# GpSimd's drain moved behind its last load, its wait for the output, and one more row on TensorE, in a batched trace of matrix products

## The chip, the cores and the metric

The kernel runs on one core of one Trainium2 chip. The time is the device time of one execution in microseconds (us). The profile is one further execution, taken by the hardware profiler; its span runs from the first to the last instruction of the program.

## The reference

For eight pairs of 2176 x 2176 matrices of float32 the reference gives the trace of each product.

```python
B, N = 8, 2176
prod = np.matmul(a, b)
traces = np.diagonal(prod, axis1=1, axis2=2).sum(axis=-1)
return traces.astype(np.float32)
```

The trace of a product is the sum over all i, k of a[i, k] * b[k, i]. So no full product is needed: A has to be transposed, multiplied with B element by element, and summed up.

## The kernel before, in words

**Data.** Each matrix is 17 blocks of 128 rows (`NT` = 17). The 17 "rows" of a tile in SBUF, counted by `v` from 0 to 16, each hold 2176 bfloat16 numbers in each of 128 partitions. Rows 0 to 4 of a matrix (`MID` = 5) go to the tile `middle`, rows 5 to 16 (two groups of `SIDE` = 6) to `a_side` or `b_side`. `middle` takes A's part first and then B's. The tile `at` takes the whole transposed A. Nearly every load is issued by GpSimd (`nc.gpsimd.dma_start`), which lets the transfer turn float32 into bfloat16; one load of batch 0 and the store of the output are issued by SyncE (lines 138 and 147).

**A batch.** GpSimd loads A's middle, then A's sides, then B's middle (line 179) and B's sides (line 187), each when the buffer is free: it waits for semaphores on which TensorE and VectorE count what they have read. TensorE (PE) transposes A by matmuls with an identity (line 305) into three PSUM tiles; ScalarE (ACT) and VectorE (DVE, every fourth tile) copy these into `at` (line 216, in `evacuate`). When `at` is full, DVE multiplies and sums in one instruction (line 229, `multiply_reduce`): `at` rows 0 to 4 with `middle`, rows 5 to 16 with `b_side`. Both give one column of `sums`, a partial sum for each partition.

**The last batch.** B's sides do not come in one load. Rows 5 to 10 are one load (line 192, semaphore `b_all`), rows 11 and 12 (`piece0`), 13 (`piece1`), 14 (`piece2`) and 15 (`piece3`) are four (line 198), and row 16 comes in three pieces (line 203): columns 768 to 2175 (`piece4`), 256 to 767 (`piece5`) and 0 to 255 (`piece6`). These are the last instructions in GpSimd's stream. The work on them is divided by hand between two engines:

- DVE (lines 271 to 284) takes rows 0 to 4, rows 5 to 8 (`DVE_ROWS` = 4), row 14 (`DVE_ROW`), columns 1024 to 2175 of row 15 (`SHARED_ROW`, from `HALF` on), and columns 768 to 1407 of row 16. Then it waits for `traced` and takes the diagonal of PE's sum with an identity (line 284).
- PE (lines 313 to 346) takes rows 9 and 10, rows 11, 12 and 13, the first 1024 columns of row 15 and the rest of row 16. For each 128 columns it multiplies a block of `at` with the block of `b_side` and adds the 128 x 128 product in `trace_ps`; the diagonal of it is the part of the trace. Between the rows some matmuls without use (`KEEP_BUSY`, after rows 10, 12, 13 and 15, into a fill tile) keep it busy. Its last real matmul raises `traced`.

At the end PE sums the columns over the partitions with a matmul by ones (line 348), DVE adds these up (line 287, semaphore `reduced`), SyncE stores the result (line 147), and the store's landing raises `out` by 16.

**The order of the work.** All of it stands in one critical section (`tc.tile_critical()`, line 135): the semaphores are written by hand, and each engine runs its instructions in the order of the code. At the end of such a section each engine drains, that is, waits until it has finished what it was given, and SyncE waits for all of these drains; the profile puts these instructions down to line 135. A second critical section (lines 352 and 353) holds nothing but SyncE's wait for `out`. Behind it come the closing barriers of the program: each engine drains and reports, GpSimd gathers the reports and releases all, semaphores are cleared, and a second such round follows. The profile puts these down to line 379.

Of the kernel before, what the change touches and what calls it, by code (L numbers as in the profile page):

```python
# [10 lines left out]
def kernel(  # L11
# [6 lines left out]
    nc = tc.nc  # L18
# [12 lines left out]
    B_GROUPS = [(0, MID), (MID * P, SIDE), ((MID + SIDE) * P, SIDE)]  # L31
    LAST = MID + SIDE

    DVE_ROWS = 4
    LATE_SLICES = [(0, 2), (2, 1), (3, 1), (4, 1)]
    DVE_ROW, SHARED_ROW = LAST + 3, LAST + 4
    HALF = 8 * P
# [25 lines left out]
    sem = {}  # L63
# [15 lines left out]
    def group(src, start, g, m):  # L79

        rows = src[start:start + P * g * m, :]
        return rows.rearrange("(g p r) k -> p g (r k)", g=g, r=m)
# [49 lines left out]
    plain = b_side.bitcast(f32).rearrange("p r k -> p (r k)")[:, :N]  # L132
    half = N // 2

    with tc.tile_critical():  # L135

        first = a[0, 0:MID * P, :].rearrange("(p r) k -> p r k", r=MID)
        nc.sync.dma_start(out=plain, in_=first[:, MID - 1, :]).then_inc(sem["first"], 16)
        for bi in range(BATCH):
# [8 lines left out]
            out=out.rearrange("(a b) -> a b", a=1), in_=result[:1, :BATCH],  # L148
# [3 lines left out]
        for bi in range(BATCH):  # L152
            last = bi == BATCH - 1
            if bi == 0:
                nc.gpsimd.dma_start(
                    out=middle[:, 0:MID - 1, :].rearrange("p r k -> p (r k)"),
                    in_=first[:, 0:MID - 1, :].rearrange("p r k -> p (r k)"),
                ).then_inc(sem["a_mid"], 16)
            else:
                nc.gpsimd.wait_ge(sem["product"], 2 * bi - 1)  # L160
                nc.gpsimd.dma_start(  # L161
                    out=middle.rearrange("p (g r) k -> p g (r k)", g=1), in_=group(a[bi], 0, 1, MID),
                ).then_inc(sem["a_mid"], 16)
                nc.gpsimd.wait_ge(sem["filled"], per_batch * bi)
            nc.gpsimd.dma_start(  # L165
                out=a_side.rearrange("p (g r) k -> p g (r k)", g=2),
                in_=group(a[bi], MID * P, 2, SIDE),
            ).then_inc(sem["a_all"], 16)
            if bi == 0:
                for t in (identity32, identity16):  # L170
                    nc.gpsimd.memset(t, 0.0).then_inc(sem["cleared"], 1)
                for k, t in enumerate((identity32, identity16)):
                    nc.gpsimd.wait_ge(sem["cleared"], 2)
                    nc.gpsimd.affine_select(
                        out=t, in_=t, compare_op=mybir.AluOpType.not_equal, fill=1.0, base=0,
                        pattern=[[-1, P]], channel_multiplier=1,
                    ).then_inc(sem["constant"], 1)
            nc.gpsimd.wait_ge(sem["filled"], per_batch * bi + mid_fills)
            nc.gpsimd.dma_start(  # L179
                out=middle.rearrange("p (g r) k -> p g (r k)", g=1), in_=group(b[bi], 0, 1, MID),  # L180
            ).then_inc(sem["b_mid"], 16)
            if bi:
                nc.gpsimd.wait_ge(sem["product"], 2 * bi)
            else:
                nc.gpsimd.wait_ge(sem["cast"], 2)
            if not last:
                nc.gpsimd.dma_start(  # L187
                    out=b_side.rearrange("p (g r) k -> p g (r k)", g=2),
                    in_=group(b[bi], MID * P, 2, SIDE),
                ).then_inc(sem["b_all"], 16)  # L190
                continue
            nc.gpsimd.dma_start(
                out=b_side[:, 0:SIDE, :].rearrange("p (g r) k -> p g (r k)", g=1),
                in_=group(b[bi], MID * P, 1, SIDE),
            ).then_inc(sem["b_all"], 16)
            rows = b[bi, LAST * P:N, :].rearrange("(p r) k -> p r k", r=SIDE)
            for k, (r, m) in enumerate(LATE_SLICES):
                nc.gpsimd.dma_start(  # L198
                    out=b_side[:, SIDE + r:SIDE + r + m, :].rearrange("p r k -> p (r k)"),
                    in_=rows[:, r:r + m, :].rearrange("p r k -> p (r k)"),  # L200
                ).then_inc(sem[f"piece{k}"], 16)
            for k, (lo, mid, hi) in enumerate(LAST_PIECES):
                nc.gpsimd.dma_start(  # L203
                    out=b_side[:, MOST - 1, lo:hi], in_=rows[:, SIDE - 1, lo:hi],
                ).then_inc(sem[f"piece{len(LATE_SLICES) + k}"], 16)


        def evacuate(engine, copy, bi, dve):
# [12 lines left out]
            out=middle[:, MID - 1, :half], in_=plain[:, :half]  # L221
# [12 lines left out]
        def rows_product(v0, rows, acc):  # L234

            m = rows.shape[1]
            return multiply_reduce(
                at[:, v0:v0 + m, :].rearrange("q v x -> q (v x)"),
                rows.rearrange("q v x -> q (v x)"), acc,
            )  # L240
# [4 lines left out]
            out=middle[:, MID - 1, half:], in_=plain[:, half:]  # L245
        ).then_inc(sem["cast"], 1)
        for bi in range(BATCH):
# [12 lines left out]
            out=result[:1, 0:BATCH - 1],  # L260
# [5 lines left out]
        def column():  # L266
            nonlocal cols
            cols += 1
            return late_acc[:, cols - 1:cols]

        rows_product(0, middle, column())
        nc.vector.wait_ge(sem["b_all"], 16 * BATCH)
        rows_product(MID, b_side[:, 0:DVE_ROWS, :], column())
        slot = SIDE - LAST
# [4 lines left out]
        for k, (lo, mid, hi) in enumerate(LAST_PIECES):  # L279
# [8 lines left out]
            out=result[:1, BATCH - 1:BATCH], in_=total[:, early:early + cols],  # L288
# [26 lines left out]
        def multiply_on_pe(landed, v, lo, hi):  # L315

            row = b_side[:, v - MID, :]
            for c in range(lo, hi, P):
                work.append((landed, at[:, v, c:c + P], row[:, c:c + P], True))
# [5 lines left out]

        for v in range(MID + DVE_ROWS, LAST):
            multiply_on_pe(("b_all", 16 * BATCH), v, 0, N)
# [21 lines left out]
            total[:, early:early + cols], ones, late_acc[:, 0:cols], start=True, stop=True,  # L349
        ).then_inc(sem["summed"], 1)  # L350

    with tc.tile_critical():
        nc.sync.wait_ge(sem["out"], 16)


# [1 line left out]
_INS = ['a', 'b']  # L357
# [26 lines left out]
```

## Time and profile before

| what | value |
|---|---|
| median of 3 runs | 712.53 us (712.15 to 712.57) |
| the profiled execution | 713.01 us |
| its span, first to last instruction | 710.9 us |
| mean granted TensorE clock | 0.655 |
| DVE busy | 382.2 us (54%) |
| PE busy | 205.3 us (29%) |
| ACT busy | 202.4 us (28%) |
| GpSimd (POOL) busy | 25.0 us (4%) |
| moved by DMA | 152.13 MB, 214 GB/s in the mean |

The profiled execution's own time is 2.1 us more than its span: that is what lies around the program. The page gives the span in 40 slices, with the busy share of each engine, of the DMA engines and the granted clock; the chain that ended last follows the work back from the last instruction that counts as work. The timeline lists instructions in order of time, with the idle time of the engine before them and what ended it. Drains, branches and semaphore instructions do not count as busy time; they are found under the line that they are put down to, with shortest, median and longest duration in ns and the first and last start in us. There an engine's name has a q (POOLq, SPq) for the engine's queue.

### The profile page before, as it was taken

What the parts mean: (1) busy time and instruction counts of PE and PEld (TensorE: products, weight loads), DVE (VectorE), ACT (ScalarE), POOL (GpSimd) and SP (SyncE); (2) the same over time, 40 slices, a digit from 0 to 9 for tenths busy, and PEclk for the clock granted to TensorE, in tenths of its full rate; (3) what the DMA queues carried; (4) which work ended last, traced back from release to release, by engine and by line L of the source; (5) the groups of instructions that cost most, each with busy time, mean ns of one, the idle gap of its engine ahead of it and who ended that gap; (6) DMA issues with size and microseconds to landing.
All of it is one profiled execution on the core that took longest, in us unless ns stands there. A gap on an engine that the chain in (4) does not pass through costs nothing. (4 is left out here: it accounts for less than half of the span.)

```text
span 710.9 us, 3916 instructions
## 1 busy us (share of the span) xinstructions
PE 205.3 (29%) x1624; PEld 186.2 (26%) x1626; DVE 382.2 (54%) x96; ACT 202.4 (28%) x158; POOL 25.0 (4%) x47
## 2 busy tenths in 40 slices
PE   0335013450134401243013520126201261013744
PEld 0334012440124301243012520126201261013732
DVE  0105488154961639616395173952739427393386
ACT  1427002370034600445004540045400472004720
POOL 1000000000000000000000000000000000002000
PEclk9859555695567855678555775567755586555878
DMA  9999999999999999999999999999999999999995
GB/s 232 215 215 220 215 207 229 215 206 226 211 215 225 211 224 214 213 224 214 220 219 213 221 216 215 220 216 208 229 212 212 226 207 222 217 211 221 217 207 100
DMA packets 7687, 152.13 MB, mean 214 GB/s; under 512 B 643, under 2 KB 899, under 8 KB 1411
## 3 DMA queue, kind: packets, MB, share of 16 engines
q0 software_dynamic: 7536, 150.96, 99.1%
q1 hardware_dynamic: 146, 1.11, 0.5%
q8 instruction: 2, 0.03, 0.0%
q14 instruction: 3, 0.02, 0.0%
HBM read 303.04 MB, written 0.00 MB: 426 GB/s over the span
## 5 line engine op out<-in xcount | busy, mean ns | idle before, releaser
L216 ACT COPY at<-fill 128x1536 bf16<-128x1536 bf16 (+3 forms) x156 | 200.0, 1371 | 472.2 <-DVE sums L229 356.7
L229 DVE CUSTOM_DVE_ANT_0 at<-at,b_side 128x26112 bf16<-128x26112 bf16 (+4 forms) x11 | 205.1, 18665 | 83.5 <-DMA b_side<-in_b_dram 83.5
L216 DVE COPY at<-fill 128x1536 bf16<-128x1536 bf16 (+2 forms) x52 | 83.9, 1614 | 221.0 <-PE fill L305 220.6
L305 PE MATMUL fill<-identity,middle 128*128 128x128 f32 (+1 forms) x440 | 68.3, 339 | 371.2 <-PEq L303 371.2
L305 PEld LDWEIGHTS fill<-identity,middle 128*128 128x128 f32 (+1 forms) x440 | 63.2, 180 | 376.1 <-issue 375.7
L305 PE MATMUL fill<-identity,a_side 128*128 128x128 f32 (+1 forms) x1056 | 123.6, 276 | 114.3 <-PEq L303 113.7
L305 PEld LDWEIGHTS fill<-identity,a_side 128*128 128x128 f32 (+1 forms) x1056 | 113.5, 167 | 124.4 <-issue 124.0
L229 DVE CUSTOM_DVE_ANT_0 at<-at,middle 128x10880 bf16<-128x10880 bf16 x8 | 91.9, 11490 | 11.0 <-ACTq L217 11.0
L179 POOL DMA_DIRECT2D middle<-in_b_dram x8 | 4.5, 562 | 334.3 <-PE fill L305 334.3
L161 POOL DMA_DIRECT2D middle<-in_a_dram x7 | 3.9, 563 | 294.4 <-DVE sums L229 294.4
L342 PE MATMUL trace_ps<-b_side,at 128*128 128x128 bf16 x105 | 8.7, 249 | 10.5 <-DMA b_side<-in_b_dram 10.4
L342 PEld LDWEIGHTS trace_ps<-b_side,at 128*128 128x128 bf16 x105 | 7.6, 115 | 12.6 <-DMA b_side<-in_b_dram 12.4
L165 POOL DMA_DIRECT2D a_side<-in_a_dram x8 | 5.7, 711 | 0.0
L187 POOL DMA_DIRECT2D b_side<-in_b_dram x7 | 5.0, 712 | 0.0
L342 PE MATMUL fill<-at 128*128 128x512 bf16 x19 | 4.8, 379 | 0.1
L244 DVE CAST middle<-b_side 128x1088 bf16<-128x1088 f32 x1 | 0.7, 727 | 5.0 <-DMA b_side<-in_a_dram 5.0
L342 PEld LDWEIGHTS fill<-at 128*128 128x128 bf16 x21 | 1.9, 98 | 1.5
L220 ACT CAST middle<-b_side 128x1088 bf16<-128x1088 f32 x1 | 1.1, 1098 | 3.9 <-DMA b_side<-in_a_dram 3.9
L198 POOL DMA_DIRECT2D b_side<-in_b_dram x4 | 2.1, 563 | 0.0
L203 POOL DMA_DIRECT2D b_side<-in_b_dram x3 | 1.6, 593 | 0.0
L220 ACT ACT_TABLE_LOAD x1 | 1.3, 1283 | 0.9 <-SPq L135 0.9
L229 DVE DVE_READ_ACCUMULATOR2_ANT sums<- 128x1 f32 x14 | 1.2, 82 | 0.0
(17 smaller groups left out, 4.2 us busy)
## 6 DMA issues: line engine op xcount, KB each, us to landing
a_side<-in_a_dram POOLq DMA_DIRECT2D x8, 6528.0 KB, 54.6
b_side<-in_b_dram POOLq DMA_DIRECT2D x7, 6528.0 KB, 52.5
middle<-in_b_dram POOLq DMA_DIRECT2D x8, 2720.0 KB, 22.2
middle<-in_a_dram POOLq DMA_DIRECT2D x7, 2720.0 KB, 24.6
b_side<-in_b_dram POOLq DMA_DIRECT2D x1, 3264.0 KB, 36.3
middle<-in_a_dram POOLq DMA_DIRECT2D x1, 2176.0 KB, 14.9
b_side<-in_b_dram POOLq DMA_DIRECT2D x3, 544.0 KB, 45.2
b_side<-in_a_dram SPq DMA_DIRECT2D x1, 1088.0 KB, 5.2
```

The costliest lines, as they stand in the source:

```text
L161: nc.gpsimd.dma_start(out=middle.rearrange("p (g r) k -> p g (r k)", g=1), in_=group(a[bi], 0, 1, MID),).then_inc(sem["a_mid"], 16)
L165: nc.gpsimd.dma_start(out=a_side.rearrange("p (g r) k -> p g (r k)", g=2), in_=group(a[bi], MID * P, 2, SIDE),).then_inc(sem["a_all"], 16)
L179: nc.gpsimd.dma_start(out=middle.rearrange("p (g r) k -> p g (r k)", g=1), in_=group(b[bi], 0, 1, MID),).then_inc(sem["b_mid"], 16)
L187: nc.gpsimd.dma_start(out=b_side.rearrange("p (g r) k -> p g (r k)", g=2), in_=group(b[bi], MID * P, 2, SIDE),).then_inc(sem["b_all"], 16)
L198: nc.gpsimd.dma_start(out=b_side[:, SIDE + r:SIDE + r + m, :].rearrange("p r k -> p (r k)"), in_=rows[:, r:r + m, :].rearrange("p r k -> p ...
L203: nc.gpsimd.dma_start(out=b_side[:, MOST - 1, lo:hi], in_=rows[:, SIDE - 1, lo:hi],).then_inc(sem[f"piece{len(LATE_SLICES) + k}"], 16)
L216: copy(out=dst, in_=src).then_inc(sem[f"free{i % BUFS}"], 1)
L220: nc.scalar.copy(out=middle[:, MID - 1, :half], in_=plain[:, :half]).then_inc(sem["cast"], 1)
L229: return nc.vector.tensor_tensor_reduce(out=x if out is None else out, in0=x, in1=y, scale=1.0, scalar=0.0, op0=MUL, op1=ADD, accum_out=acc,)
L244: nc.vector.tensor_copy(out=middle[:, MID - 1, half:], in_=plain[:, half:]).then_inc(sem["cast"], 1)
L305: done = nc.tensor.transpose(into, block, identity)
L342: done = nc.tensor.matmul(trace_ps if real else fill_tiles[0][:, 0:4, :], x, y, start=(n == 0 or not real), stop=(n == len(work) - 1 or no ...
```

## The change

The change has two parts. `DVE_ROWS` goes from 4 to 3, so row 8 of the last batch is multiplied by PE, as its first row behind the wait for `b_all` (line 326), and no longer by DVE (line 273). And the end is arranged anew: the section is told not to drain GpSimd (`no_gpsimd_drain=True`), GpSimd gets a drain and a wait for `out` of its own behind its last load, and the second section with SyncE's wait goes away.

```diff
-    DVE_ROWS = 4
+    DVE_ROWS = 3
...
-    with tc.tile_critical():
+    with tc.tile_critical(no_gpsimd_drain=True):
...
                 nc.gpsimd.dma_start(
                     out=b_side[:, MOST - 1, lo:hi], in_=rows[:, SIDE - 1, lo:hi],
                 ).then_inc(sem[f"piece{len(LATE_SLICES) + k}"], 16)
+        nc.gpsimd.drain()
+        nc.gpsimd.wait_ge(sem["out"], 16)
...
-    with tc.tile_critical():
-        nc.sync.wait_ge(sem["out"], 16)
-
```

## The prediction, made before the changed kernel ran

> **What bounds the kernel now.** I read the page first, then the chain that ended last, then the timeline of the last 25 us, and last the instructions behind the kernel's last line, which count as no work and so hardly stand on the page. The page says what the first 700 us hang on.
>
> ```profile
> span 710.9 us, 3916 instructions
> DMA  9999999999999999999999999999999999999995
> GB/s 232 215 215 220 215 207 229 215 206 226 211 215 225 211 224 214 213 224 214 220 219 213 221 216 215 220 216 208 229 212 212 226 207 222 217 211 221 217 207 100
> ```
>
> Every slice but the last has the DMA engines busy at 90% or more. So up to the last landing at 702.95 us (semaphore events of the trace) no engine's work counts but what delays a load; the change moves no load. It can only act behind the last loads, and there are two pieces of that. The first is DVE's, from the chain (start us, us, what):
>
> ```profile
> 691.42 9.14 DVE at L229
> ...
> 700.57 2.34 DVE at L229
> ...
> 702.92 1.27 DVE at L229
> ...
> 704.20 0.74 DVE at L229
> ...
> 704.94 0.20 DVE diagonal L229
> ```
>
> These are the products of rows 5 to 8 (8704 elements a partition), row 14 (2176), 1152 columns of row 15, 640 columns of row 16, and the diagonal of PE's sum. They follow one another without a gap, although the data are there earlier: piece2 landed at 697.64, piece3 at 700.21, piece4 at 701.92, and PE had finished ("traced") at 703.30. DVE is 1.5 us behind everything it waits for.
>
> The second piece lies behind the output's issue at 705.62. The chain ends there, but the span has 5.3 us more. The instructions put down to the section's line 135 say why (duration ns min/median/max, first and last start):
>
> ```profile
> L135 SPq NOP  x2: 13/13/13, 0.7 to 709.3; - x2
> L135 ACTq DRAIN  x1: 14/14/14, 706.0 to 706.0; - x1
> L135 POOLq DRAIN  x1: 3250/3250/3250, 706.0 to 706.0; - x1
> L135 DVEq DRAIN  x1: 19/19/19, 706.0 to 706.0; - x1
> ```
>
> All engines drain at 706.0, when SyncE has issued the output; ACT and DVE take 0.02 us, GpSimd 3.25. SyncE's waits name it as well: "SPq L135" waited 3.0 us for "POOLq L135", once. Meanwhile the output landed at 706.68, 1.06 us after its issue (semaphore events), so its wait costs nothing now. Then come the second section and the closing barriers:
>
> ```profile
> L379 POOLq DRAIN  x3: 34/34/112, 709.3 to 710.7; - x3
> L379 SPq DRAIN  x3: 7/7/7, 710.0 to 710.3; - x3
> ```
>
> GpSimd's next drain, right behind the long one, takes 34 ns: the long one's work is done once. SyncE comes through the second section from 709.37 to 710.0 (its lines 352 and the barrier's first SyncE drain), and from its arrival at the barrier to the last instruction it is 710.1 to 710.9, 0.82 us.
>
> **Part 1, row 8 to TensorE.** DVE loses 2176 of 8704 elements. Slope of the chain's rows: (9.14 - 2.34) / (8704 - 2176) = 1.042 ns an element, so three rows take 9.14 - 2.27 = 6.87 us. Step by step: row 14 starts at 691.42 + 6.87 = 698.29 (piece2 is there since 697.64); row 15's part at 700.63 (piece3 at 700.21); that ends at 701.90, when piece4 is just landing, 701.92, with some 0.05 for the wait 701.97; row 16's part ends at 702.71. Now PE is late: "traced" comes at 703.30, and the diagonal starts at 703.34 where it started at 704.86. Of 2.27 us taken from DVE, 1.52 come out at the end.
>
> PE gains 17 matmuls and as many weight loads, between row 8's place and row 9, behind the same wait for b_all (687.2).
>
> ```profile
> 687.22 3.72 PE L342 MATMUL trace_ps<-b_side,at 128*128 128x128 bf16 x34 [7.50 <-DMA b_side<-in_b_dram]
> 690.99 1.46 PE L342 MATMUL fill<-at 128*128 128x512 bf16 x6
> 693.06 2.07 PE L342 MATMUL trace_ps<-b_side,at 128*128 128x128 bf16 x34 [0.61 <-DMA b_side<-in_b_dram]
> ...
> 700.26 0.62 PE L342 MATMUL trace_ps<-b_side,at 128*128 128x128 bf16 x8 [1.59 <-DMA b_side<-in_b_dram]
> ```
>
> The granted clock is 0.54 in 687.2 to 691.0 and 1.00 after 691; 34 matmuls take 3.72 us at the one and 2.07 at the other. Seventeen more cost 1.04 to 1.86 us. Idle time in front of piece0 (0.61) and piece3 (1.59 by the timeline) is 2.2 us together, so even the dearer figure is gone by 700.26: it costs nothing at the end. What follows 700.26 is paced by the landings of pieces 3 to 6. If that cover were gone, each us that PE comes late at "traced" would be one us at the end. Bounds of part 1: 0 (PE late by 1.5) and 1.52 (PE can't end before piece6, which landed at 702.95).
>
> **Part 2, the drain and the sections.** Moved: one GpSimd drain, from 706.0 to behind the last load's issue, which ends at 654.57 + 0.60 = 655.2. It stands in front of nothing but the new wait: GpSimd issues no load after it, so it is moved past no queue's work. Added: GpSimd's wait for the output. Behind that wait stand GpSimd's share of the section's end and of the closing barriers, and every engine waits for those. Removed: the section's 3.25 us drain and the second section, 0.64 us of SyncE.
>
> How long the early drain takes no row shows. At the short end it has done its work for the earlier loads long before 703 and ends with the last landing, 702.95, or a little behind it; at the long end it starts its 3.25 us only there and ends at 706.2. A gain below nothing is excluded for the drain itself: no load waits for it, so its start can bring nothing forward. I take the short end: the long drain of before ran when all had landed for 3.07 us, so its time is work of GpSimd's own and no waiting, and 47.8 us lie between 655.2 and 702.95 to do it in. Either way GpSimd then waits for the output.
>
> Sum: the output is issued at 705.62 - 1.52 = 704.10 and lands 1.06 later, 705.16. From there through GpSimd's wake-up and SyncE's arrival at the barrier I estimate 0.25 us (GpSimd's semaphore instructions at the end stand 0.08 apart, SyncE's 0.07; three or four of them; bounds 0.1 and 0.4), and 0.82 to the end: 706.2 against 710.9. That is 4.7 us, of which part 1 has 1.5 and part 2 3.2.
>
> The profiled execution took 713.01 us, 2.1 more than its span, which I leave as it is: 708.3. The runs shown have a median of 712.53 us, 0.5 less; by those 712.53 - 4.7 = **707.8 us**.
>
> **A rule against the change.** In the trace GpSimd's issues at 562.45 and 563.00 took 562 and 711 ns beside a DVE copy that took its usual 1491, so neither held the other; a drain beside a DVE instruction does not occur. The Trainium skill, "SBUF — State Buffer", summary of rules for kernel authors, says that of a DVE operation with two SBUF inputs and a GpSimd operation that reads SBUF the later one fully blocks until the first is done. If a waiting drain counted as such an operation, DVE's products would be held until 703 and the time would be that of the fourth rival; if it does not, the sum above stands. The drain's row is listed under GpSimd's queue and names no tile, which speaks for the second.
>
> **Rivals.** One: the drain's 3.25 us begin only with the last landing. It ends at 706.2, 1.04 behind the output, and the same 0.25 + 0.82 follow: span 707.3, time 708.9. For it: one drain is all the trace has, and it ran after all landings. Against it: its length shows no waiting.
>
> Two: the drain's cost comes back, because the closing barrier's drain, which now follows GpSimd's wait, pays it again. Then 705.16 + 0.1 + 3.25 + 0.1 + 0.82 = 709.4, a gain of 1.5: 711.0. Against it: the 34 ns of the second drain.
>
> Three: part 1 gives nothing, as PE comes 1.5 us later. That needs the slow clock for longer: at 0.54 all through, the 51 matmuls take 51 x 0.109 = 5.6 us and the next 34 another 3.7. Then only part 2's 3.2 us remain: 709.3. Against it: the clock rose at 691 under the same load.
>
> Four, the one that ends slower: the drain holds DVE. From 655.2 on DVE has 4 x 1.76 + 0.96 us of copies and 11.4 + 6.9 + 2.3 + 1.3 + 0.7 of products, 31 us, nearly all of which would run behind 703: a span of about 736, a time of about 737. For it: no row shows a drain beside a DVE instruction. Against it: GpSimd's issue and DVE's copy at 562 went side by side at their usual lengths. It decides from the point where DVE is held over 4.7 us longer than the loads hold it.
>
> **How the numbers follow.** Forecast 0.71; one 0.13; two 0.05; three 0.07; four 0.04. The forecast's own bounds are 707.5 (0.1 us in place of 0.25, and a few hundredths) to 708.0 (0.4), and runs of before scatter by 0.4. The range 707.2 to 709.2 holds the forecast and rival one, 0.84; rival three's 709.3 is just outside. A measurement can tell 0.2%, 1.4 us, from no change. Faster by that: the forecast, one, three and half of two, 0.94; within it the other half of two, 0.02; slower 0.04.
>
> **What would show it.** Right: no long GpSimd drain behind the output's issue, the drain at 655.2 ending near 703, no instruction of a second section, DVE's diagonal at 703.3 and behind a wait for PE, the output issued at 704.1, 2.1 us from there to the span's end. PE's idle time before piece3 shrinks, the landings stay. Wrong: a drain that ends at 706 (one), a long drain in the closing barrier (two), "traced" well behind 703.3 (three), or DVE's copies behind 655 starting late (four).

## The result, and the profile after

The changed kernel takes 708.68 us (median of 6 runs, 708.49 to 709.28) against 712.55 (712.15 to 713.08, 6 runs). The ratio is 0.9945 with a 95% interval of 0.9933 to 0.9958: 3.9 us less, between 3.0 and 4.8. The forecast was 707.8 with a range of 707.2 to 709.2. The profiled execution took 708.71 us with a span of 706.6.

The chain that ended last (start us, us, what) no longer runs through DVE's products. From the last loads on it is this ("issue" is time in which the engine waited for nothing that the profile shows):

```profile
652.90 49.87 DMA b_side<-in_b_dram
702.77 0.05 issue
702.82 0.69 PE trace_ps L344 x6
703.51 0.02 issue
703.53 0.29 DVE diagonal L231
...
703.88 0.21 PE total L350 x2
704.09 0.02 issue
704.12 0.15 DVE result L289
```

The loads, PE on the last pieces as they land, and then the few short steps that can't begin earlier. DVE's timeline says the same from its side; the brackets hold its idle time and what ended it:

```profile
691.21 6.95 DVE L231 CUSTOM_DVE_ANT_0 at<-at,b_side 128x6528 bf16<-128x6528 bf16 x1
...
698.09 2.42 DVE L231 CUSTOM_DVE_ANT_0 at<-at,b_side 128x2176 bf16<-128x2176 bf16 x1
...
702.14 0.83 DVE L231 CUSTOM_DVE_ANT_0 at<-at,b_side 128x640 bf16<-128x640 bf16 x1 [0.34 <-DMA b_side<-in_b_dram]
...
703.53 0.29 DVE L231 CUSTOM_DVE_ANT_0 diagonal<-identity,trace_ps 128x128 bf16<-128x128 f32 x1 [0.56 <-PE trace_ps L344]
```

The product of three rows takes 6.95 us where that of four took 9.22, and DVE now waits twice: 0.34 us for piece4, 0.56 us for PE. On PE:

```profile
687.06 5.30 PE L344 MATMUL trace_ps<-b_side,at 128*128 128x128 bf16 x51 [7.49 <-DMA b_side<-in_b_dram]
692.42 1.46 PE L344 MATMUL fill<-at 128*128 128x512 bf16 x6
693.71 2.06 PE L344 MATMUL trace_ps<-b_side,at 128*128 128x128 bf16 x34
...
700.46 0.62 PE L344 MATMUL trace_ps<-b_side,at 128*128 128x128 bf16 x8 [1.14 <-DMA b_side<-in_b_dram]
```

With row 8, PE's first rows take 5.30 - 3.72 = 1.58 us more. The idle time in front of piece0's rows is gone, and that in front of piece3's has become 1.14 us; PE is still ahead of the loads.

Behind the output's issue (704.29) the instructions of the section's line are (duration ns min/median/max, first and last start us):

```profile
L135 SPq NOP  x2: 13/13/13, 0.7 to 705.6; - x2
...
L135 POOLq NOP  x1: 13/13/13, 705.5 to 705.5; - x1
```

In GpSimd's place in the section's end stands a NOP (an instruction that does nothing) of 13 ns instead of a drain of 3250. GpSimd's drain is found under its own line, and its drains in the closing barriers are short:

```profile
L206 POOLq DRAIN  x1: 52200/52200/52200, 652.6 to 652.6; - x1
...
L378 POOLq DRAIN  x3: 34/41/112, 705.6 to 706.3; - x3
```

By the record it lasts from 652.61 to 704.81. Its start can't be taken to the tenth: the last load's issue, which stands before it in the stream, is recorded only from 653.42 to 654.02. What follows rests on its end alone. The last piece landed at 703.17 and the output at 705.36 (semaphore events), so the drain ends 1.64 us behind the last load and 0.55 us before the output is there.

### The profile page after: what moved, and what is told of

Read it like the earlier page. It is cut to its first block, busy times and chain, and to the rows that moved or that the text cites. A ratio compares the mean times of both kernels' runs of the same rounds, so it can differ in the third digit from the quotient of the medians.

```text
span 706.6 us, 3944 instructions
## 1 busy us (share of the span) xinstructions
PE 207.3 (29%) x1641; PEld 188.0 (27%) x1643; DVE 380.2 (54%) x96; ACT 202.3 (29%) x158; POOL 25.0 (4%) x47
## 3 DMA queue, kind: packets, MB, share of 16 engines
q0 software_dynamic: 7536, 150.96, 99.7%
## 5 line engine op out<-in xcount | busy, mean ns | idle before, releaser
L231 DVE CUSTOM_DVE_ANT_0 at<-at,b_side 128x26112 bf16<-128x26112 bf16 (+4 forms) x11 | 202.9, 18460 | 84.1 <-DMA b_side<-in_b_dram 84.1
L344 PE MATMUL trace_ps<-b_side,at 128*128 128x128 bf16 x122 | 10.3, 253 | 9.4 <-DMA b_side<-in_b_dram 9.3
L344 PEld LDWEIGHTS trace_ps<-b_side,at 128*128 128x128 bf16 x122 | 9.3, 116 | 11.3 <-DMA b_side<-in_b_dram 10.9
```

Of the source, the lines that this page charges most:

```text
L231: return nc.vector.tensor_tensor_reduce(out=x if out is None else out, in0=x, in1=y, scale=1.0, scalar=0.0, op0=MUL, op1=ADD, accum_out=acc,)
L344: done = nc.tensor.matmul(trace_ps if real else fill_tiles[0][:, 0:4, :], x, y, start=(n == 0 or not real), stop=(n == len(work) - 1 or no ...
```

## The experiments

**The two parts alone.** First row 8 on TensorE with the old end:

```diff
-    DVE_ROWS = 4
+    DVE_ROWS = 3
```

> The kernel before with row 8 of the last batch on TensorE, its end left as it was. My theory: the two parts add up, and this part is worth what the last landing allows. In the changed kernel the diagonal starts at 703.5 where before had 704.9, so 1.3 us less: about 711.2 us against 712.5, the 3.25 us drain following the output's issue as before. Rival: the long drain's end hangs on the last landing (it ended 6.3 us behind it before), so an earlier output gains nothing: 712.5.

Measured: 711.46 us against 712.72, ratio 0.9984 (0.9975 to 0.9994), 1.3 us less. The diagonal waits for PE, the output is issued at 704.48, and the section's drain moved with it:

```profile
703.72 0.29 DVE L229 CUSTOM_DVE_ANT_0 diagonal<-identity,trace_ps 128x128 bf16<-128x128 f32 x1 [0.55 <-PE trace_ps L342]
...
L135 POOLq DRAIN  x1: 3250/3250/3250, 704.9 to 704.9; - x1
```

Its length is the same, and it ended 4.8 us behind the last landing (703.35) where it ended 6.3 us behind it before. So it does not hang on the last landing. The rival falls.

This run also shows how thin PE's cover is. The granted clock was 0.50 from 687.5 to 693.2, so all 51 matmuls of rows 8 to 10 ran at the slow clock and took 5.62 us, as rival three supposed for them; 0.30 us of PE's idle time were left in front of piece3's rows.

Then the new end with four rows on DVE:

```diff
-    DVE_ROWS = 3
+    DVE_ROWS = 4
```

> The changed kernel with rows 5 to 8 on DVE again. My theory: the output is issued at 705.6 and lands at 706.7 as before, the early drain is over by then, and the changed kernel's 0.39 + 0.78 us follow: span 707.9, 3.0 us less than before, about 709.5 us. Rival (the drain still holds the end for some of its time): 710.5 or more.

Measured: 709.89 us, ratio 0.9958 (0.9945 to 0.9972), 2.8 us less; span 708.0 where 707.9 was expected. The output lands at 706.77 and the span ends 1.21 us later, as in the changed kernel. The rival falls. The two parts together, 1.3 + 2.8 = 4.1 us, are what both give at once, 3.9, within the intervals.

**Which piece of the new end does it?** Only the drain is added to the kernel before:

```diff
                 ).then_inc(sem[f"piece{len(LATE_SLICES) + k}"], 16)
+        nc.gpsimd.drain()
```

> The kernel before with nothing but GpSimd's own drain added behind its last load; the section's own drain, the second section and row 8 on DVE stay. My theory: the section's drain shrinks to some 0.04 us, SyncE comes to its wait for the output before 706.68, and 1.35 us follow from there as before: span 708.0, 2.9 us less, about 709.6 us. So the second section is worth only some 0.2 us. Rival (each section's drain pays its 3.25 us anew): 712.5, no change.

Measured: 709.98 us, ratio 0.9959 (0.9946 to 0.9973), 0.4 us above the expected figure, with a span of 708.1 where 708.0 was expected. The section's own drain, still there, has nothing left to do:

```profile
L135 POOLq DRAIN  x1: 41/41/41, 706.1 to 706.1; - x1
```

So one added line has all of part 2 that the times can tell. By the profiles the span ends 1.34 us behind the output's landing here and 1.21 with the new end: the second section and SyncE's wait are worth 0.13 us.

The counterpart takes only this line out of the changed kernel:

```diff
-        nc.gpsimd.drain()
         nc.gpsimd.wait_ge(sem["out"], 16)
```

> The changed kernel without its own drain behind the last load; GpSimd only waits for the output. My theory: the drain's work is then paid by the closing barrier, and behind the output's landing, not beside it: 3.2 us more than the changed kernel, span about 709.7, about 711.9 us, with a GpSimd drain of about 3.25 us at line 378 or so. Rival (the cost belongs to the section's kind of drain, and the closing one is short as always): 708.7, like the changed kernel.

Measured: 711.57 us (712.72 before, ratio 0.9985, 0.9976 to 0.9994), 2.9 more than the changed kernel. The closing barrier now pays; its GpSimd drains are:

```profile
L377 POOLq DRAIN  x3: 40/112/3250, 705.4 to 709.3; - x3
```

The longest of the three is the first; it begins 0.27 us behind the output's landing (705.18). This kernel is no better than row 8 alone (711.46): leaving out the section's drain gains nothing by itself. In each of these runs the next drain in GpSimd's stream pays, whichever it is.

**What the drain's length is made of.** These runs are read for their drains and landings; each is one execution. Four batches in place of eight, the old end (the result's tile keeps its eight places and is set to zero first):

```diff
-    BATCH, N, N2 = a.shape
+    ALL, N, N2 = a.shape
+    BATCH = 4
...
```

> The kernel before with four batches in place of eight (the last four traces are left at zero), so 23 loads on GpSimd's queue in place of 39 and about half the bytes; the old end. It is for the length of the section's GpSimd drain alone. A price for each load (3.25 us / 39 = 0.083) gives 1.9 us; a price by bytes or descriptors 1.6 us; a fixed price 3.25 us.

```profile
L136 POOLq DRAIN  x1: 1938/1938/1938, 356.6 to 356.6; - x1
```

The same bytes in more loads:

```diff
-            nc.sync.wait_ge(sem["a_all"], 16 * (bi + 1))
+            nc.sync.wait_ge(sem["a_all"], 32 * (bi + 1))
...
-            nc.gpsimd.dma_start(
-                out=a_side.rearrange("p (g r) k -> p g (r k)", g=2),
-                in_=group(a[bi], MID * P, 2, SIDE),
-            ).then_inc(sem["a_all"], 16)
+            for g in range(2):
+                nc.gpsimd.dma_start(
+                    out=a_side[:, g * SIDE:(g + 1) * SIDE, :].rearrange("p (g r) k -> p g (r k)", g=1),
+                    in_=group(a[bi], (MID + g * SIDE) * P, 1, SIDE),
+                ).then_inc(sem["a_all"], 16)
```

> The kernel before with each load of A's sides split into two loads: 47 loads in place of 39, the same bytes; the old end. For the length of the section's GpSimd drain. A price for each load gives 3.9 us; a price by bytes, or a fixed one, 3.25 us.

```profile
L135 POOLq DRAIN  x1: 3903/3903/3903, 706.1 to 706.1; - x1
```

23, 39 and 47 loads give 1.938, 3.250 and 3.903 us: (3.250 - 1.938) / 16 = 0.082 and (3.903 - 3.250) / 8 = 0.082 us for each load, and 0.05 on top. Bytes and a fixed price are out. So is a price by packets: GpSimd's queue moved 7536 with 39 loads and 7664 with 47, 2% more, and the drain is 20% longer.

A drain in the middle, in front of batch 4's first load:

```diff
                 nc.gpsimd.wait_ge(sem["product"], 2 * bi - 1)
+                if bi == BATCH // 2:
+                    nc.gpsimd.drain()
```

> The kernel before with one more GpSimd drain in the middle, in front of batch 4's first load, when 16 of the 39 loads have been issued; the old end. For the length of the section's drain. If a drain's price counts only the loads since the drain before, 23 x 0.082 + 0.05 = 1.94 us; if it counts all loads of the program, 3.25 us again. The drain in the middle waits for batch 3's last load and holds batch 4's first load back, so the time itself should be some 2 to 4 us longer, by a gap in the loads.

```profile
L135 POOLq DRAIN  x1: 1930/1930/1930, 710.5 to 710.5; - x1
```

Only the 23 loads since the drain before count. The one in the middle (from 341.98 on) ended at 354.20, 0.70 us behind the only load that was still under way (353.50). The time, 716.13 us beside 713.11 in one run each, shows what such a drain costs where loads stand behind it: some 3 us. The output was issued 4.4 us later (710.11 for 705.74), and the shorter drain at the end gave 1.3 us back.

**The early drain's remainder.** The changed kernel with four batches:

> The changed kernel with four batches in place of eight (the last four traces are left at zero). For the early drain's end: it came 1.64 us behind the last landing in the changed kernel. If that remainder is a fixed price behind the last landing, 1.6 us again; if it is a part of a price that grows with all the loads, about half, 0.8 us; if it belongs to the last loads alone (nine in flight), 1.6 us too.

Its drain ended at 355.03, 0.99 us behind the last landing at 354.05. So the remainder belongs neither to the last loads, which are the same, nor is it fixed. With the drain in the middle there are three points, 16, 23 and 39 loads with 0.70, 0.99 and 1.64 us: 0.041 us for each load. About half of a drain's price can't be done early; it comes behind the last landing and grows with all loads since the drain before, those included that had long landed. (The expected 0.8 us was half of 1.64 us; by the loads it should have been 23/39 of it, 0.97.) The test is to make that remainder longer than the output's way:

```diff
-            nc.sync.wait_ge(sem["a_all"], 16 * (bi + 1))
+            nc.sync.wait_ge(sem["a_all"], 64 * (bi + 1))
...
-            nc.gpsimd.dma_start(
-                out=a_side.rearrange("p (g r) k -> p g (r k)", g=2),
-                in_=group(a[bi], MID * P, 2, SIDE),
-            ).then_inc(sem["a_all"], 16)
+            for g in range(2):
+                side = a[bi, (MID + g * SIDE) * P:(MID + (g + 1) * SIDE) * P, :].rearrange(
+                    "(p r) k -> p r k", r=SIDE)
+                for r0 in (0, SIDE // 2):
+                    r1 = r0 + SIDE // 2
+                    nc.gpsimd.dma_start(
+                        out=a_side[:, g * SIDE + r0:g * SIDE + r1, :].rearrange("p r k -> p (r k)"),
+                        in_=side[:, r0:r1, :].rearrange("p r k -> p (r k)"),
+                    ).then_inc(sem["a_all"], 16)
```

> The changed kernel with each load of A's sides split into four: 63 loads in place of 39, the same bytes. My theory: a remainder of 0.042 us for each load is paid behind the last landing even by the early drain, so it ends 63 x 0.042 = 2.65 us behind it in place of 1.64, about 705.8, and that is 0.5 us behind the output's landing: now the drain holds the end, and the span is about 0.5 us longer than the changed kernel's with the same last landing. Rival (the 1.64 us belong to the last nine loads): the drain ends 1.64 us behind the last landing as before and the span keeps 706.5.

```profile
L211 POOLq DRAIN  x1: 53174/53174/53174, 653.5 to 653.5; - x1
```

It ended at 706.72, 2.62 us behind the last landing (704.10) and 0.43 behind the output's (706.29). The span ended 1.66 us behind the output's landing where the changed kernel has 1.21: the drain holds the end, by 0.45 us. The time was 710.03 us. The last landing itself came 0.9 us later than in the changed kernel; this delay was already there at the landing of the last batch's first load (628.91 for 627.96), before the drain began.

**Is DVE still last?** One more row goes to TensorE in the changed kernel:

```diff
-    DVE_ROWS = 3
+    DVE_ROWS = 2
```

> The changed kernel with one more row, row 7, on TensorE (rows 5 and 6 on DVE). My theory: DVE is no longer last; the diagonal waits for PE, and PE for the last landing. So no change against the changed kernel: 708.7 within 0.2 us. Rival (DVE's length still counts): up to 2.3 us less, 706.4. If PE becomes too late by its 17 further matmuls: more than 709.

Measured: 708.63 us (708.62 to 708.82), no change against 708.68. DVE now waits for its data already in front of row 14, and in front of the diagonal it waits longer than with three rows (0.69 us for 0.56):

```profile
697.67 2.43 DVE L231 CUSTOM_DVE_ANT_0 at<-at,b_side 128x2176 bf16<-128x2176 bf16 x1 [2.07 <-DMA b_side<-in_b_dram]
...
703.44 0.29 DVE L231 CUSTOM_DVE_ANT_0 diagonal<-identity,trace_ps 128x128 bf16<-128x128 f32 x1 [0.69 <-PE trace_ps L344]
```

**The kernel before once more**, for a second profile:

> The kernel before, unchanged, for a second profile of it. If its first profiled execution, 713.01 us, was a long one by chance, this one lies nearer to the median, with a span of about 710.5 us and a last landing some tenths earlier; the drain again 3.25 us.

Measured: 713.11 us, span 711.0, last landing 703.02, drain 3250 ns. The execution was as long as the first profiled one, so my expectation missed: two profiles of long executions don't show what a short one does differently. In 21 runs of this kernel the spans go from 710.3 to 711.2 and the times are 1.9 to 2.1 us above them, so its scatter lies inside the span. (Not so the longest run of the changed kernel, 709.28 us: its span is 706.4.)

## Why the prediction was right, and where its terms were off

**Part 1** held as worked out. DVE's chain ended before PE's, the diagonal waited for "traced" and started at 703.53 (703.34 forecast), and the output was issued at 704.29 (704.10). Both 0.19 us come from one thing: piece6 landed at 703.17 and not at 702.95, 0.22 us later; it lies between 702.95 and 703.35 in the eight profiles whose loads are those of before. That DVE is no longer the bound is shown by the kernel with two rows on DVE; in its trace too the diagonal starts 0.4 us behind the last landing (703.44 and 703.03). PE's cover held: row 8 cost 1.58 us, between the forecast's 1.04 and 1.86. It was thinner than the forecast had it, which took the granted clock to rise at 691 as in its trace: in row 8 alone it was still 0.50 up to 693.2, and 0.30 us were left.

**Part 2, the drain.** The mechanism was right in the main: what a drain behind the last load's issue has done is not paid again at the end. The step on its end was wrong at both ends that it offered. I took the drain to end with the last landing or a little behind it, and kept 3.25 us behind it as the long end; it ended 1.64 us behind it. The reason given ("its time is work of GpSimd's own and no waiting, and 47.8 us lie there to do it in") holds for half of it only. What the two halves do no trace shows. It cost nothing, because the output's way from the last landing to its own, 2.2 us (703.17 to 705.36), is longer; the kernel with 63 loads shows the price when it isn't. The forecast had not worked out this margin of 0.55 us, so that the time did not suffer was luck in this step.

**Part 2, the exit.** From the output's landing to the end I had 0.25 + 0.82 us; it took 1.21. GpSimd's branch with the wait starts at 705.38, its NOP only at 705.54; this 0.16 us from the one to the other was not among the steps of 0.07 to 0.08 us that I counted. The barrier began at 705.75, so the 0.25 were 0.39, just within the bounds of 0.1 and 0.4.

**The sum.** The span is 706.57 where 706.2 was forecast: 0.2 by the landing, 0.14 by the exit. Between the two profiled executions the gain is 713.01 - 708.71 = 4.3 us where 4.7 was forecast. Between the medians it is 3.9. The remaining 0.4 is the step from the profiled execution to the median: before's lay 0.46 us above the median of its 6 runs, the changed kernel's 0.03 above. I took the gain of a long execution whole from the median. Both errors made the forecast too low, by 0.9 us in all. The measured 708.68 lies above the forecast's own bounds (708.0) and within the range only because that was made to hold rival one (708.9). Where a short execution saves its tenths stays open, as told above.

**The rivals.** One (3.25 us begin with the last landing) came half true in its mechanism and not in its price. Two (the closing barrier pays again) does not happen in the changed kernel, whose closing drain takes 41 ns, but it is exactly what happens without the added drain. Three fell with PE's rows: its condition came about for rows 8 to 10 in row 8 alone, and even there PE was in time. Four fell with DVE's, of which these are two, first of the changed kernel beside the long drain, then of the kernel before:

```profile
661.92 1.76 DVE L218 COPY at<-fill 128x1536 bf16<-128x1536 bf16 x1 [12.98 <-PE fill L307]
...
679.80 11.48 DVE L231 CUSTOM_DVE_ANT_0 at<-at,middle 128x10880 bf16<-128x10880 bf16 x1
...
662.08 1.76 DVE L216 COPY at<-fill 128x1536 bf16<-128x1536 bf16 x1 [12.99 <-PE fill L305]
...
679.94 11.48 DVE L229 CUSTOM_DVE_ANT_0 at<-at,middle 128x10880 bf16<-128x10880 bf16 x1
```

The copy and the product of rows 0 to 4 took to the hundredth what they took before. The rule that was weighed against the change (the Trainium skill, "SBUF — State Buffer", summary of rules for kernel authors) thus does not reach the drain in this trace, although the product has two inputs in SBUF; why, no run shows.

## What to carry to other kernels

Look behind the last instruction that counts as work: the chain of the profile ended at the output's issue, but two thirds of this change's gain (2.8 of 4.1 us) came out of the 5.3 us behind it, and what fills them is named only by the list of instructions under the section's line and by SyncE's waits. A GpSimd drain pays for each load since the last drain, so put one behind the last load, where nothing is queued behind it, and check that its remainder ends before the output lands. When a shortened engine stops being last, forecast the next wait, not the time taken from the engine: 2.27 us taken from DVE gave 1.3. Subtract a profile's gain from that profile's own time; carrying it to a median adds that execution's distance from it as an error.

## What the runs showed of the hardware that was not expected

In these runs GpSimd's drain costs 0.082 us for each load that its queue issued since the drain before, and 0.05 us on top, whatever the bytes (23, 39, 47 loads: 1.94, 3.25, 3.90 us), even when all have landed some 3 us earlier. A drain that is issued while the last of them are under way still ends behind the last landing, by 0.041 us for each load since the drain before and 0.04 us on top (16, 23, 39, 63 loads: 0.70, 0.99, 1.64, 2.62 us); with 16 loads, only one was still under way.
